# Delta-net substitution: its steps on GpSimd instead of VectorE, and the order they share with the key pages

## The chip, the cores and the metric

One core of a Trainium2 chip runs the whole kernel. The metric is the device time in microseconds (us), the median of several runs. The engines are named as the profile names them: PE is TensorE (matmuls), PEld its weight loads, DVE is VectorE, ACT is ScalarE, POOL is GpSimd, SP is SyncE, which only issues transfers here. ACTq and SPq are the transfer queues of ACT and SP.

## The reference, cut to what matters

One layer of a decoder: a normalised input goes through one projection, whose columns feed three kinds of heads (differential attention over paged keys and values, a state space model, a gated delta net) and their gates; the mixed result goes through an output projection. The change concerns the delta net, four heads of 128 over 1024 positions:

```python
lower = jnp.where(strict, beta[..., :, None] * kk * decay, 0.0)
rhs = jnp.concatenate([v * beta[..., None], k * (beta * jnp.exp(g_cum))[..., None]], axis=-1)
sol = lax.linalg.triangular_solve(lower + eye, rhs, left_side=True, lower=True, unit_diagonal=True)
u, w = sol[..., :DV_C], sol[..., DV_C:]
```

and, in the attention of the eight sample rows, the logits of a query against 4096 past keys each, which lie in pages of 128:

```python
logits = jnp.einsum('bqhmd,bkhmd->bmhqk', q, k).astype(jnp.float32) * (DH_A ** -0.5)
```

## The kernel before

**Stages.** From 0 to about 850 us the input projection runs (L458 in `proj_fm`). Each weight tile is split into a high part (`whi`, cast on ACT, L155) and a low part (`wlo`, a subtraction on POOL, L201), and each 128 columns of output take 72 matmuls in three pieces of positions, three for each of eight slices: high times high, high times low, low times high. The buffers of the split weights are three half tiles deep (`WB = 3`). Beside this run the sample attention (key and value pages stream in on SP's queue) and the delta-net heads 1 to 3. From 860 to 1100 us follow the prompt attention, head 4 of the delta net and the state space model, then the output projection (L1833).

**Key pages.** `k_pages` loads two pages into a tile `kt` (`KB = 3` buffers), multiplies them with the query on POOL (L842, four products of 128x256) and sums them on DVE (L843) into `lg`. `page_softmax` (L853, L858 and others, PE and DVE) follows when all pages of a sample are in, and `v_mul` (L898) multiplies value pages `vt` with the weights `wz`.

**A delta-net head** (`gdn_head`). The triangular system is solved for chunks of 128 positions. `LT` holds the matrices. Their 32x32 blocks on the diagonal are stored to memory (`invd`) and loaded again as `Dm`, one block to each partition group's row (L1131 to L1134, on ACT's queue). Then 31 steps invert them by substitution in the tile `U`: a product with a row of `Dm` into `tv`, and a subtraction, each on DVE through the helper `tt` (L159). `U` is stored (L1151) and loaded back into `LT` (L1154), again on ACT's queue, and PE goes on from there: transposes (L1163), the off-diagonal blocks (L1175 to L1199), the right-hand sides (L1207, L1208), and the recurrence over eight chunks (L1220 to L1226).

**What sets the order.** The kernel is written as generators that are advanced in turn by the cost they yield, and a planner then reorders the instructions of each engine by a timeline of its own. One rule is written by hand: `gstep` holds the last step written so far, and what `k_pages` issues inside `behind_gdn()` on the engine of that step is ordered behind it (`tc.issue_after` adds an order on one engine, no wait between engines). While the steps are on DVE, these are the reductions L843. An engine runs its instructions in the planned order.

Of the kernel before, what the change touches and what calls it, by code (L numbers as in the profile page):

```python
# [14 lines left out]
ALU = mybir.AluOpType  # L15
# [63 lines left out]
def bl(ap, n):  # L79
    return ap.unsqueeze(len(ap.shape)).broadcast_to(list(ap.shape) + [n])  # L80


def bm(ap, n):
    return ap.unsqueeze(1).broadcast_to([ap.shape[0], n] + list(ap.shape[1:]))
# [3 lines left out]
def trunk_kernel(  # L88
# [47 lines left out]
    def unit(shape, dt=F32, n="u"):  # L136
        return up.tile(shape, dt, tag="u", name=nm(n))

    def half(shape=(P, 512), dt=F32, n="h"):
        return hp.tile(list(shape), dt, tag="h", name=nm(n))  # L140
# [9 lines left out]
    def small(shape, n, dt=F32, bufs=2):  # L150
        return sp.tile(shape, dt, tag=n, name=nm(n), bufs=bufs)
# [6 lines left out]
    def tt(out, a, b, op):  # L158
        return V.tensor_tensor(out=out, in0=a, in1=b, op=op)  # L159
# [3 lines left out]
    def tte(e, out, a, b, op):  # L163
        return EN[e].tensor_tensor(out=out, in0=a, in1=b, op=op)
# [877 lines left out]
    def gdn_head(h):  # L1042
# [89 lines left out]
        Dm = unit([P, 32, 32], n="Dm")  # L1132
# [3 lines left out]
        U = half([P, 16, 32], n="U")  # L1136
# [6 lines left out]
        for j in range(31):  # L1143
            n, m = 31 - j, j // 4 + 1
            tv = U[:, 8:16].rearrange("p a b -> p (a b)")[:, 0:m * n].rearrange("p (c i) -> p c i", i=n)
            tt(tv, bl(U[:, 0:m, j], n), bm(Dm[:, j, j + 1:32], m), ALU.mult)
            step = tt(U[:, 0:m, j + 1:32], U[:, 0:m, j + 1:32], tv, ALU.subtract)
            gstep[:] = [step.ins]
            yield 0.5
        for g in range(4):  # L1150
# [86 lines left out]
        m = small([P, 8], "sm")  # L1237
# [370 lines left out]
    def gdn_all():  # L1608
        for h in range(4):
            while len(graw.get(h, ())) < 3:  # L1610
                yield 0.5
            yield from gdn_head(h)
# [58 lines left out]
    for b in range(32):  # L1671
        n = bk.count(b)
# [271 lines left out]
```

## Time and profile before

| | us |
|---|---|
| median of 3 runs | 1275.63 |
| lowest, highest | 1272.66, 1278.05 |
| profiled execution | 1270.58 |
| its span in the trace | 1268.8 |
| PE busy in the span | 1136.3 (90%) |
| DVE busy | 833.6 (66%) |
| POOL busy | 643.8 (51%) |
| ACT busy | 471.6 (37%) |

The profiled execution is one run of the same program; its stretches are read in us from the start of the span. PE is the engine with the most work. Its clock varies: the granted clock of the whole span is 0.947 of full speed in the mean. The four heads substitute at about 276 to 322, 481 to 532, 688 to 732 and 900 to 940 us.

### The profile page before, as it was taken

To read this page: it belongs to the slowest core of one execution; us is meant where nothing else is said; L and a number is where in the kernel's file an instruction comes from. 1 tells how busy PE (TensorE), PEld (TensorE's weight loads), DVE (VectorE), ACT (ScalarE), POOL (GpSimd) and SP (SyncE) were. 2 spreads that over 40 slices of the span, in tenths; PEclk is the share of its full clock that TensorE was granted. 3 is DMA by queue.
4 is the path that set the end of the run, shared out by engine and by line. 5 is a ranking of instruction groups with operands and counts; after the bars stand their busy time and mean duration, and the time that the engine had idled before them with its cause. 6 is when DMAs were issued, how large, how long until landed. Compare 5 with 4: busy or idle time off the path is not lost.

```text
span 1268.8 us, 22346 instructions
## 1 busy us (share of the span) xinstructions
PE 1136.3 (90%) x7365; PEld 959.4 (76%) x7365; DVE 833.6 (66%) x1994; ACT 471.6 (37%) x998; POOL 643.8 (51%) x779
## 2 busy tenths in 40 slices
PE   4999999989889988888997799988899999799997
PEld 3799887768669777867866688866568778678876
DVE  6723698549478658945754955787878988664444
ACT  6332223211114332233353233436737759341111
POOL 3747867646665653573965778772023251341100
PEclk9999999989789988898988899998998999899999
DMA  8646765994884962696797599999786664961420
GB/s 298 200 164 205 238 208 161 349 324 134 280 293 155 319 214 77 190 333 211 234 318 226 183 322 336 307 287 257 219 225 174 161 167 133 299 198 52 131 69 34
DMA packets 246452, 275.57 MB, mean 217 GB/s; under 512 B 31905, under 2 KB 163376, under 8 KB 246322
## 3 DMA queue, kind: packets, MB, share of 16 engines
q1 hardware_dynamic: 168082, 214.44, 52.3%
q10 hardware_dynamic: 78256, 59.72, 16.4%
q8 instruction: 58, 0.95, 0.3%
q14 instruction: 56, 0.46, 0.1%
HBM read 231.59 MB, written 42.67 MB: 216 GB/s over the span
## 4 chain that ended last, share of the span: by engine, by line
PE 53%; DMA 16%; DVE 15%; issue 5%; ACT 3%; SPq 3%; POOL 3%; ACTq 1%; DVEq 0%; POOLq 0%
PE b L458 23%; PE b L1833 10%; PE pv L898 4%; DMA kt<-in_cache_k_dram 3%; DVE U L159 3%; DMA vt<-in_cache_v_dram 3%; DMA w<-in_w_in_dram 2%; DVE lg L843 2%; DVE cy L167 2%; PE b L745 1%; SPq L823 1%; POOL kt L842 1%; PE b L1893 1%; DVE e L721 1%; DMA zb<-zfd 1%
## 5 line engine op out<-in xcount | busy, mean ns | idle before, releaser
L458 PE MATMUL b<-hh,whi 128*128 128x344 f32 (+1 forms) x2016 | 508.6, 335 | 23.0 <-DVE cy L167 11.6
L842 POOL TENSOR_TENSOR kt<-kt,qb 128x256 f32<-128x256 f32 x512 | 364.5, 745 | 159.8 <-DMA kt<-in_cache_k_dram 104.0
L458 PEld LDWEIGHTS b<-hh,whi 128*128 128x128 f32 x2016 | 363.7, 197 | 56.0 <-issue 30.1
L458 PE MATMUL b<-hh,wlo 128*128 128x344 f32 (+1 forms) x1008 | 332.4, 334 | 3.5 <-POOL wlo L201 3.5
L843 DVE TENSOR_REDUCE lg<-kt 128x16 f32<-128x1024 f32 x128 | 154.6, 1211 | 88.0 <-POOL kt L842 85.2
L458 PEld LDWEIGHTS b<-hh,wlo 128*128 128x128 f32 x1008 | 197.1, 196 | 15.7 <-issue 10.1
L201 POOL TENSOR_TENSOR wlo<-w,whi 128x512 fp32r<-128x512 f32 x86 | 111.1, 1297 | 92.9 <-ACT whi L155 80.5
L1833 PE MATMUL b<-wo,mh 128*128 128x512 f32 (+1 forms) x408 | 121.7, 380 | 0.2 <-POOL wo L1567 0.2
L155 ACT ACTIVATE whi<-w 128x512 fp32r<-128x512 f32 x86 | 54.1, 631 | 160.8 <-PE b L458 114.4
L167 DVE SCALAR_TENSOR_TENSOR cy<-b,vec,cy 128x341 f32<-128x341 f32 (+4 forms) x180 | 99.0, 563 | 1.5 <-DVE U L159 0.2
L898 PE MATMUL pv<-vt,wz 128*32 128x512 f32 x512 | 78.3, 645 | 22.6 <-DMA vt<-in_cache_v_dram 15.0
L1833 PEld LDWEIGHTS b<-wo,mh 128*128 128x128 f32 x408 | 74.6, 188 | 14.5 <-POOL wo L1567 0.4
L1833 PE MATMUL b<-wo,ml 128*128 128x512 f32 (+1 forms) x204 | 77.1, 378 | 0.0
L1801 POOL TENSOR_TENSOR ml<-zt,mh 128x512 fp32r<-128x512 f32 x16 | 22.4, 1404 | 104.7 <-ACT mh L1800 104.5
L159 DVE TENSOR_TENSOR U<-U,Dm 128x60 f32<-128x60 f32 (+24 forms) x124 | 40.6, 327 | 18.7 <-DMA Dm<-invd 16.8
L156 ACT ACTIVATE e<-e,nmx 128x128 f32<-128x128 f32 (+7 forms) x64 | 48.9, 766 | 8.8 <-DVE nmx L723 5.4
L155 ACT ACT_TABLE_LOAD x33 | 42.3, 1283 | 25.5 <-DMA qh<-qfd 8.5
L718 PE MATMUL b<-kTh,qh 128*128 128x128 f32 (+3 forms) x96 | 41.1, 431 | 11.7 <-DVE mx L721 6.5
L159 DVE TENSOR_TENSOR y<-b,gate 128x512 f32<-128x512 f32 (+1 forms) x17 | 11.1, 658 | 54.2 <-PE b L1833 54.2
L1833 PEld LDWEIGHTS b<-wo,ml 128*128 128x128 f32 x204 | 38.3, 188 | 7.3
L971 DVE TENSOR_SCALAR cy<-b,vec 128x344 f32<-128x344 f32 (+1 forms) x60 | 33.2, 564 | 14.5 <-PE b L458 14.3
L898 PEld LDWEIGHTS pv<-vt,wz 128*32 128x32 f32 x512 | 12.4, 110 | 39.6 <-issue 18.9
(531 smaller groups left out, 2022.9 us busy)
## 6 DMA issues: line engine op xcount, KB each, us to landing
kt<-in_cache_k_dram SPq DMA_DIRECT2D x256, 256.0 KB
vt<-in_cache_v_dram SPq DMA_DIRECT2D x256, 256.0 KB
w<-in_w_in_dram ACTq DMA_DIRECT2D x82, 256.0 KB
zfd<-zf ACTq DMA_DIRECT2D x12, 512.0 KB
wo<-in_w_out_dram SPq DMA_DIRECT2D x12, 512.0 KB
om<-mixd SPq DMA_DIRECT2D x24, 256.0 KB
xt<-in_x_prompt_dram SPq DMA_DIRECT2D x8, 512.0 KB
hx<-in_w_ada_dram SPq DMA_DIRECT2D x16, 256.0 KB
```

The costliest lines, as they stand in the source:

```text
L155: return S.activation(out, in_, func, bias=bias, scale=scale)
L156: return S.activation(out, in_, func, bias=bias, scale=scale, accum_out=accum)
L159: return V.tensor_tensor(out=out, in0=a, in1=b, op=op)
L167: return V.scalar_tensor_tensor(out=out, in0=a, scalar=s, in1=b, op0=op0, op1=op1)
L201: G.tensor_tensor(out=lo, in0=w32, in1=hi.bitcast(F32), op=ALU.subtract)
L458: TE.matmul(ps[:, 0:N], a, b[k][:, sl], start=(i == 0), stop=(i == 23))
L718: TE.matmul(ps[:, 0:b - a], qh[:, m, ts], kT[m][:, a:b], start=True, stop=False)
L842: G.tensor_tensor(out=kt[:, j, c], in0=kt[:, j, c], in1=qb[:, c], op=ALU.mult)
L843: V.tensor_reduce(out=lg[:, 2 * g:2 * g + 2, :], in_=kt.rearrange("p j (a d) -> p j a d", d=64), axis=AX.X, op=ALU.add)
L898: mm = TE.matmul(pv[32 * r:32 * r + 32, :], wz[:, 2 * g + j, :], vt[:, j, :], start=(b == 0 and g < 2), stop=(b == NS - 1 and g >= 14 and ...
L971: V.tensor_scalar_mul(y[:, c0_:c0_ + m], ps[:, o:o + m], wv[3])
L1833: TE.matmul(ps[c], m[a][:, kt % 4, :], w[kt][:, c[0]:c[1]], start=(kt == KT[0] and i == 0), stop=(kt == KT[-1] and i == 2))
```

## The change

The two instructions of each of the 31 steps are issued through the helper `tte` (L164) with engine "g", so on POOL, with the same operands: 248 instructions in four heads. `gstep` then holds an instruction of POOL, and what `behind_gdn()` orders behind it are the products L842 in the place of the reductions L843. Nothing else is written differently.

```diff
@@ -1143,8 +1143,8 @@
         for j in range(31):
             n, m = 31 - j, j // 4 + 1
             tv = U[:, 8:16].rearrange("p a b -> p (a b)")[:, 0:m * n].rearrange("p (c i) -> p c i", i=n)
-            tt(tv, bl(U[:, 0:m, j], n), bm(Dm[:, j, j + 1:32], m), ALU.mult)
-            step = tt(U[:, 0:m, j + 1:32], U[:, 0:m, j + 1:32], tv, ALU.subtract)
+            tte("g", tv, bl(U[:, 0:m, j], n), bm(Dm[:, j, j + 1:32], m), ALU.mult)
+            step = tte("g", U[:, 0:m, j + 1:32], U[:, 0:m, j + 1:32], tv, ALU.subtract)
             gstep[:] = [step.ins]
             yield 0.5
```

The planner answers with another order on all engines. On POOL, in head 1's substitution, the row before is this (`wlo` are low halves of weights, `kt` key pages, numbers tell tiles apart, `kN` is a scaling of the head's keys):

```order
L201 TENSOR_TENSOR wlo_3659<-w_473_3624,whi_3658 128x512
L842 TENSOR_TENSOR kt_3439<-kt_3439,qb_3265 128x256 x4
L201 TENSOR_TENSOR wlo_3746<-w_474_3626,whi_3745 128x512
L842 TENSOR_TENSOR kt_3500<-kt_3500,qb_3265 128x256 x4
L201 TENSOR_TENSOR wlo_3912<-w_502_3877,whi_3911 128x512
L842 TENSOR_TENSOR kt_3566<-kt_3566,qb_3265 128x256 x4
```

and now, near the end of the head's steps:

```order
L842 TENSOR_TENSOR kt_3268<-kt_3268,qb_3265 128x256 x4
L164 TENSOR_TENSOR U_2837<-U_2837,Dm_2832 128x48
L201 TENSOR_TENSOR wlo_3746<-w_474_3626,whi_3745 128x512
L164 TENSOR_TENSOR U_2837<-U_2837 128x6x8
L164 TENSOR_TENSOR U_2837<-U_2837,Dm_2832 128x49
L201 TENSOR_TENSOR wlo_3912<-w_502_3877,whi_3911 128x512
L164 TENSOR_TENSOR U_2837<-U_2837 128x7x7
L164 TENSOR_TENSOR U_2837<-U_2837,Dm_2832 128x42
L164 TENSOR_TENSOR U_2837<-U_2837 128x7x6
L164 TENSOR_TENSOR U_2837<-U_2837,Dm_2832 128x35
L164 TENSOR_TENSOR U_2837<-U_2837 128x7x5
L842 TENSOR_TENSOR kt_3357<-kt_3357,qb_3265 128x256 x4
```

The low halves and the products have moved in among the steps; behind wlo_3912 there are 15 more steps and the products of kt_3357 up to the head's last step. In head 2, wlo_5527 stands behind 26 steps in the same way.

On PE, where head 3's chain begins (`b` are accumulators; L458 is the projection, `pv` the products of value pages), the row before is

```order
L458 MATMUL b_8566<-hh_514,wlo_8393 128x344
L458 MATMUL b_8566<-hh_525,whi_8392 128x344
L1163 MATMUL b_8155<-ident,LT_7281 128x128 x4
L1163 MATMUL b_8163<-ident,LT_7281 128x128 x4
L898 MATMUL pv<-vt_8396,wz 32x512 x2
L898 MATMUL pv<-vt_8408,wz 32x512 x2
L458 MATMUL b_8566<-hh_526,whi_8392 128x344
L458 MATMUL b_8566<-hh_525,wlo_8393 128x344
```

and now

```order
L458 MATMUL b_8721<-hh_773,wlo_8478 128x344
L898 MATMUL pv<-vt_8076,wz 32x512 x2
L898 MATMUL pv<-vt_8144,wz 32x512 x2
L898 MATMUL pv<-vt_8222,wz 32x512 x2
L898 MATMUL pv<-vt_8338,wz 32x512 x2
L1163 MATMUL b_8155<-ident,LT_7281 128x128 x4
L1163 MATMUL b_8163<-ident,LT_7281 128x128 x4
L1175 MATMUL b_8202<-T_973_7472,LT_7281 32x32 x4
L1176 MATMUL b_8203<-T_973_7472,LT_7281 32x32 x4
```

The transposes L1163 have moved from behind 2620 to behind 2688 matmuls of L458, and the chain from L1163 to L1226 now stands in a row, with products of value pages but no projection matmuls between. In head 1 the transposes stand behind 1176 matmuls of L458 in both orders, and the chain stood in a row there already.

## Rows read from the trace of the kernel before

**Rows 1.** The page, busy us (share of the span) and instructions of two engines.

```profile
PE 1136.3 (90%) x7365; PEld 959.4 (76%) x7365; DVE 833.6 (66%) x1994; ACT 471.6 (37%) x998; POOL 643.8 (51%) x779
```

**Rows 2.** The page, the chain that ended last, share of the span by line.

```profile
PE b L458 23%; PE b L1833 10%; PE pv L898 4%; DMA kt<-in_cache_k_dram 3%; DVE U L159 3%; DMA vt<-in_cache_v_dram 3%; DMA w<-in_w_in_dram 2%; DVE lg L843 2%; DVE cy L167 2%; PE b L745 1%; SPq L823 1%; POOL kt L842 1%; PE b L1893 1%; DVE e L721 1%; DMA zb<-zfd 1%
```

**Rows 3.** Windows: stretch, length, busy us by engine, granted clock, DMA share, GB/s.

```profile
core 0: us, PE busy (x) PEld busy (x) DVE busy (x) ACT busy (x) POOL busy (x), PEclk, DMA share, GB/s
276.00:322.00 46.00, 43.90 (x265) 36.41 (x258) 41.06 (x112) 7.76 (x13) 20.52 (x24) 1.00 0.64 200
332.00:368.00 36.00, 25.62 (x215) 15.79 (x213) 17.21 (x28) 8.27 (x21) 23.43 (x33) 0.70 0.85 295
481.00:532.00 51.00, 46.41 (x265) 43.94 (x266) 47.23 (x127) 10.79 (x14) 22.78 (x26) 0.88 0.38 118
692.00:732.00 40.00, 31.59 (x167) 29.89 (x166) 38.30 (x86) 10.20 (x16) 27.20 (x31) 0.83 0.61 194
732.00:760.00 28.00, 28.00 (x255) 23.77 (x253) 12.37 (x15) 11.75 (x23) 23.84 (x30) 1.00 1.00 324
900.00:940.00 40.00, 35.44 (x242) 22.39 (x242) 34.29 (x162) 16.35 (x47) 4.54 (x8) 1.00 0.82 241
```

**Rows 4.** Windows of tile U alone, four heads' substitutions: sum and mean.

```profile
sum 181.00, DVE 77.05 POOL 0.00; mean DVE 19.26 POOL 0.00
```

**Rows 5.** Timeline of DVE: start, us, line, operation [idle before <- releaser].

```profile
276.19 0.18 DVE L159 TENSOR_TENSOR U<-U,Dm 128x31 f32<-128x31 f32 x1
...
321.15 0.16 DVE L159 TENSOR_TENSOR U<-U 128x8 f32<-128x8 f32 x1
...
481.21 0.19 DVE L159 TENSOR_TENSOR U<-U,Dm 128x31 f32<-128x31 f32 x1 [2.64 <-DMA Dm<-invd]
...
688.07 0.19 DVE L159 TENSOR_TENSOR U<-U,Dm 128x31 f32<-128x31 f32 x1 [14.15 <-DMA Dm<-invd]
...
731.14 0.17 DVE L159 TENSOR_TENSOR U<-U 128x8 f32<-128x8 f32 x1
...
936.95 0.68 DVE L159 TENSOR_TENSOR pvs<-pv,hm 128x512 f32<-128x512 f32 x1
```

**Rows 6.** Timeline of PE: its stops on DVE, and head 1's and 3's transposes.

```profile
317.60 0.55 PE L458 MATMUL b<-hh,whi 128*128 128x344 f32 x2 [1.57 <-DVE U L159]
...
334.20 1.06 PE L1163 MATMUL b<-ident,LT 128*128 128x128 f32 x8 [1.83 <-DMA LT<-invd]
...
511.16 0.91 PE L458 MATMUL b<-hh,whi 128*128 128x344 f32 x2 [3.37 <-DVE cy L167]
...
700.24 0.27 PE L853 MATMUL b<-ident,smx 128*8 128x128 f32 x1 [2.02 <-DVE U L159]
...
709.59 0.59 PE L858 MATMUL b<-sdg,ones 8*128 8x8 f32 x2 [3.62 <-DVE sdg L857]
...
727.45 1.08 PE L898 MATMUL pv<-vt,wz 128*32 128x512 f32 x8 [2.78 <-DVE wz L159]
...
749.33 1.03 PE L1163 MATMUL b<-ident,LT 128*128 128x128 f32 x8
```

**Rows 7.** Groups of POOL by form: count, busy us, mean ns, idle before.

```profile
L842 POOL TENSOR_TENSOR kt<-kt,qb 128x256 f32<-128x256 f32 x512 | 364.5, 745 | 159.8 <-DMA kt<-in_cache_k_dram 104.0 <-DVE U L159 12.8 <-DMA qb<-qd 10.7
L201 POOL TENSOR_TENSOR wlo<-w,whi 128x512 fp32r<-128x512 f32 x86 | 111.1, 1297 | 92.9 <-ACT whi L155 80.5 <-PE b L1119 9.7 <-PE b L458 1.4
```

**Rows 8.** Timeline of POOL: a memset and two small copies.

```profile
938.27 0.31 POOL L1497 MEMSET gwz<- 128x256 f32 x1 [1.96 <-PE b L1501]
938.64 0.33 POOL L1499 COPY gwz<-gWQ 128x8 f32<-128x8 f32 x2
```

**Rows 9.** Windows of line L458 alone on PE: matmuls up to two times.

```profile
0.00:743.00 743.00, 463.56 (x2588) 0.93 0.72 232
0.00:316.50 316.50, 194.29 (x1104) 0.97 0.71 228
```

**Rows 10.** Timeline of ACT and its queue: the store of U in head 1.

```profile
321.35 2.64 ACTq L1151 DMA_DIRECT2D invd<-U  x4
```

## What I expect, and how I come to it

> **What bounds the kernel now.** I read the busy shares first. TensorE is busy for 90% of the span, GpSimd for 51% [rows 1], so the time is that of TensorE's work plus the places where it stands still or runs at its lower clock. The chain of work that ended last, by line, puts 23% on the projection matmuls L458 and only 3% on the steps (VectorE, tile U, L159) [rows 2]: some 40 us of 1268.8 are at stake in the steps, and not all of that can be had.
>
> The busy time by stretches says where. While heads 1, 2 and 3 substitute (276 to 322, 481 to 532, 692 to 732 us), VectorE is busy 41.06 of 46, 47.23 of 51 and 38.30 of 40 us: it is the tight engine there. GpSimd has 20.52, 22.78 and 27.20 us of work in the same stretches, so it isn't idle either [rows 3]. The steps themselves take 77.05 us of VectorE in four heads, 19.26 each [rows 4], and from first to last step a head takes about 45 us, because VectorE does other work between them (276.19 to 321.15 in head 1 [rows 5]).
>
> **What the change takes off VectorE.** The waits of TensorE that name VectorE in the three stretches are the gain. Head 1: one wait of 1.57 us on a step. Head 2: 3.37 us on the convolution's VectorE work, which stands in the queue between steps [rows 6], and 2.64 us in which VectorE itself stood at the first step, waiting for Dm, with convolution work queued behind it [rows 5]. Head 3: 2.02, 3.62 and 2.78 us, all three in the page softmax and its weights, whose VectorE work stands among steps [rows 6]; sum 8.4. Each such stop is followed by matmuls at a lower granted clock: it is 0.83 over 692 to 732 and 0.88 over 481 to 532, against 1.00 where nothing stops [rows 3]. A mean of 0.83 between the two levels (1.2 and 2.4 GHz) is a third of 40 us, 13 us, at the low one, where a matmul takes nearly twice as long; that loses about 6 us in head 3, and I take 2 in head 2, where part of the low clock comes from a stop that stays. Gains: head 1 1.6, head 2 2.64 + 3.37 + 2 = 8.0, head 3 8.4 + 6 = 14.4. Head 4's steps (in 900 to 940) are half of VectorE's 34.29 us there, and TensorE is idle for 4.6 of 40 us [rows 3]; I take half, 2 us. All gains: 26 us.
>
> **What a step costs on GpSimd.** No row shows a small two-input instruction there. The nearest are the products of 256 elements a partition at 745 ns and the low halves of weights (wlo, L201) of 512 at 1297 ns [rows 7]; the line through both is 2.16 ns an element and 193 ns. The 62 instructions of a head have 50 elements in the mean (31 steps of (31-j) columns by j//4+1): 302 ns. A copy that follows a memset starts 0.06 us after the memset's end (938.27 + 0.31 to 938.64) [rows 8], and every step waits for the one before, so 0.36 us and 62 x 0.36 = 22.4 us a head. From below: two copies of 8 elements took 0.33 us [rows 8], 0.17 each, with the gap 0.23, 14.3 us a head. From above: twice VectorE's 19.26 us, 38.5 us a head, 0.62 each. I take 0.36, since it is read off the same operation on the same engine, and keep the ends.
>
> **What the steps stand between on GpSimd.** With the new order, from the first step of a head to its last GpSimd also runs 23, 27 and 41 instructions of its other work, by the mean times of their groups 21.6, 24.6 and 39.3 us (products, wlo, kN, in head 3 the state's products too). With 22.4 us of steps that is 44.0, 47.0 and 61.7 us from first to last. VectorE needed 45.0 (276.19 to 321.15) in head 1 and 43.1 (688.07 to 731.14) in head 3 [rows 5]. The steps haven't become shorter, then; in head 3 they end later by 18.6 us, at 749.8.
>
> **Head 1.** GpSimd runs in order, so each wait of its other work now holds the substitution. wlo_3912 stands with 15 steps and the products of kt_3357 behind it. Its buffer comes free when TensorE ends the 1104th matmul of L458; in the trace that is at 316.50 [rows 9]. From there 1.3 (wlo) + 4 x 0.745 + 15 x 0.36 = 9.7 us: the last step at 326.2, where it was 321.3. Then U is stored and LT loaded back: the store is issued at 321.35 [rows 10], and the transposes L1163 begin at 334.20, 12.9 us after the last step, already waiting for LT by 1.83 us [rows 6]. Nothing covers a delay there: +4.9 us, which takes the 1.57 us with it. By the low price of a step it is +3.0; by the high one the sum of the work decides, 276.2 + 21.6 + 38.5 = 336.3, +15.
>
> **Head 2.** The steps end by 47.0 us after 481.2, earlier than before, so LT isn't late. But wlo_5527 stands behind 26 of the steps, and TensorE's matmuls on it with it: between nothing and 26 x 0.36 = 9.4 us, depending on how far GpSimd is ahead of TensorE there, which no row settles. I take half: 8.0 gained, 4.7 lost, -3.3.
>
> **Head 3.** U's end at 749.8 and 12.9 us for the way through memory give LT at 762.7. In the trace L1163 runs at 749.33 behind 2620 matmuls of L458 [rows 6], and 2588 of them had run by 743 [rows 9], 0.20 us each with all that stands between; in the new order 2688 stand ahead of it, 68 more, 13.6 us. Less the 14.4 us gained TensorE gets there at 748.5 and waits 14.2 us. Behind it the whole chain of head 3 now stands in a row, without projection matmuls between its members. Head 1 shows what this costs: over 332 to 368 us, where its chain runs so, TensorE is busy 25.62 of 36 us at a granted clock of 0.70, while head 3's, which is interleaved now, runs with 28.00 of 28 us busy at 1.00 [rows 3]. So 10 us are lost that aren't lost now (the clock, which would add to it, I leave out, and keep it for the range). Head 3: -14.4 + 14.2 + 10 = +9.8.
>
> **The order rule.** The rule that held VectorE's reductions L843 behind the last step written ahead of them now holds GpSimd's products L842 there; both stand on the engine of the steps, so no wait across engines is added, only places in a queue (counted above). The reductions are free of it, which may hand key buffers back to the page loads on SP's queue sooner; against that stand products that come later in head 3, where the DMA share is 1.00 in 732 to 760 already [rows 3]. I put no number on either.
>
> **Sum:** 4.9 - 3.3 + 9.8 - 2 = +9.4 us on the profiled execution's 1270.58, 1280.0. That execution lies 5.05 us below the median of the three runs, 1275.63; on the median the forecast is 1285.0.
>
> **The rivals.**
> 1. Faster: GpSimd is quick on small tiles and the wait at L1163 is short. At 0.23 us a step: head 1 +3.0; head 2 -8.0, nothing late; head 3 ends at 688.1 + 39.3 + 14.3 = 741.7, LT at 754.6, a wait of 6.1 us and, with the clock kept up, half the 10 us: -3.3; head 4 -2. Sum -10.3: 1265. For it speaks that the 8-element copies are that short; against it, the line through the same operation and that the wait on wlo_3912 doesn't depend on a step's price. It decides if U of head 3 ends by about 742 us in terms of the old trace.
> 2. No change: the price is 0.36, but ScalarE's cast for wlo_3912 comes early enough (head 1: 0) and the serial block of head 3 loses 5 us less: 0 - 3.3 + 4.8 - 2 = -0.5, 1275. For it: pv products stand between the members of that block and fill some of it.
> 3. Much slower: the steps cost 0.62 us. Head 1 +15; head 2 -8.0 + 26 x 0.62 / 2 = 0; head 3: U at 688.1 + 39.3 + 38.5 = 765.9, LT at 778.8, a wait of 30.3 us, +25.9; head 4 -2. Sum +39: 1315. The 38.5 us are twice the trace's 19.26, in which contention with GpSimd is already contained [rows 4]; the line through the two rows on GpSimd [rows 7] speaks against it.
>
> On rival 3 there is a rule. The Trainium skill, "GPSIMD Engine Reference", section 4.1 Engine selection, names VectorE for elementwise work on a tile and puts GpSimd at about twice its time for operations with two inputs. At 512 elements the trace agrees: VectorE took 0.68 us for a product [rows 5], GpSimd 1.297 us for wlo [rows 7]; no row shows it at 50 elements. By the rule the time would be rival 3's, 1315.
>
> **How the numbers follow.** Forecast 0.40, rival 1 0.22, rival 2 0.25, rival 3 0.13. About 0.5% (6 us) is what a measurement of this kernel can tell from no change. The forecast and rival 3 are slower by more than that (0.53), rival 1 faster (0.22), rival 2 within it (0.25). The range reaches into rival 1, to 1261, and to just short of rival 3's full price, 1312; what is left out is about half of each, 0.18.
>
> **What would show it.** The mean distance of two steps on GpSimd in the profile after: 0.36 right, 0.25 rival 1, 0.6 rival 3. TensorE's wait at L1163 for LT: about 7 us in head 1 and 14 in head 3 if I am right, 2 and 6 by rival 1. TensorE's waits on VectorE in the page softmax of head 3 should be gone, and its granted clock in the step stretches near 1.00. The chain should show GpSimd's steps L164 in head 3 in the place of VectorE's L159. The forecast is wrong if GpSimd's own waits (on pages, on ScalarE's casts) stand still less than I think, or if the time lost in head 3's block comes back in the page stream that has to end anyway.

## The result: 1.3% slower

| | before | after |
|---|---|---|
| median, us (4 runs each) | 1276.84 | 1291.06 |
| lowest, highest | 1272.66, 1281.92 | 1290.51, 1294.70 |
| profiled execution | 1270.58 | 1290.51 |
| its span | 1268.8 | 1288.8 |

The ratio is 1.0126, with an interval of 1.0091 to 1.0160. The two profiled executions are 20 us apart, the medians 14; the kernel before varies by some 10 us from run to run, and its profiled one is a quick one. So a difference read from the two traces may be 6 us too large.

The page of the kernel after, its busy shares and its chain by line (to be read against [rows 1, 2]):

```profile
PE 1142.6 (89%) x7365; PEld 959.1 (74%) x7365; DVE 771.3 (60%) x1746; ACT 469.9 (36%) x997; POOL 720.3 (56%) x1027
...
PE b L458 24%; PE b L1833 10%; DMA vt<-in_cache_v_dram 4%; PE pv L898 4%; POOL kt L842 2%; DVE lg L843 2%; DMA kt<-in_cache_k_dram 2%; POOL U L164 2%; DVE cy L167 1%; PE b L745 1%; POOL wlo L201 1%; SPq L823 1%; ACT e L156 1%; DMA hx<-in_w_ada_dram 1%; PE b L1893 1%
```

VectorE has lost 62 us of work and GpSimd gained 76; on the chain the steps now stand as POOL U L164, and the key products on GpSimd rose to 2%. The stretches of the kernel after (columns as in [rows 3]): head 1's steps and the block behind them, head 2's steps, head 3's steps and the block behind them.

```profile
279.00:327.00 48.00, 48.00 (x290) 41.37 (x290) 25.86 (x50) 11.50 (x16) 39.55 (x87) 1.00 0.58 181
334.00:372.00 38.00, 24.43 (x202) 16.85 (x206) 17.43 (x24) 6.36 (x17) 25.28 (x36) 0.59 0.86 287
478.00:536.00 58.00, 52.59 (x313) 47.62 (x314) 38.16 (x78) 16.29 (x22) 45.10 (x95) 0.94 0.38 113
690.00:751.00 61.00, 57.12 (x349) 54.87 (x348) 25.39 (x42) 22.82 (x33) 56.82 (x104) 0.97 0.54 167
751.00:791.00 40.00, 30.12 (x236) 19.76 (x237) 15.88 (x18) 10.28 (x23) 32.42 (x46) 0.66 0.94 307
```

While a head substitutes, TensorE runs as it was meant to: busy 48.00 of 48 and 57.12 of 61 us, its granted clock 0.94 to 1.00. GpSimd is the full engine now, 56.82 of 61 us in head 3. What is lost is lost behind the steps: 751 to 791 us, 30.12 of 40 us busy at a clock of 0.66, where the kernel before ran with 28.00 of 28 at 1.00 [rows 3]. Of the 9.88 us in which TensorE stands there, nearly all lie ahead of the block, before 763.37; in the block itself it is busy for 26.48 of 27.63 us, and what it lacks is the clock. The two parts in the kernel after, and below them the times of the second in the kernel before:

```profile
751.00:763.37 12.37, 3.64 (x17) 0.42 (x17) 3.66 (x3) 0.63 (x1) 12.37 (x18) 0.58 0.88 248
763.37:791.00 27.63, 26.48 (x224) 19.33 (x221) 12.21 (x15) 9.65 (x22) 20.05 (x30) 0.69 0.98 334
```

```profile
763.37:791.00 27.63, 27.63 (x209) 24.43 (x207) 15.31 (x22) 10.51 (x19) 23.19 (x30) 1.00 1.00 337
```

Where in the program the time goes is seen best by counting the projection's matmuls (L458), as [rows 9] does. The time at which each was reached, in whole us:

| matmul of L458 | before | after | difference |
|---|---|---|---|
| 1176 (before head 1's block) | 332 | 330 | -2 |
| 1200 (behind it) | 373 | 381 | +8 |
| 1560 (shortly before head 2's steps) | 460 | 469 | +9 |
| 1992 (head 2 done) | 584 | 585 | +1 |
| 2400 (early in head 3's steps) | 697 | 698 | +1 |
| 2688 | 767 | 751 | -16 |
| 2712 (behind head 3's block) | 778 | 791 | +13 |
| 3024 (the last is the 3048th) | 843 | 859 | +16 |

In each head the steps' stretch gains, and the block behind it takes more than that back in heads 1 and 3. The count flatters the gain at the 2688th, though: the kernel before has by then also run 104 matmuls of head 3's chain and 32 of value pages that the kernel after still has ahead of it. They take 7.5 us in the trace before, so of the 17 us from the 2400th to the 2688th about 9 are gained, and 7.5 of what the block loses is work that was only moved. TensorE in the kernel after, at the two blocks (start us, us, line, operation [idle before <- releaser]):

```profile
337.93 1.30 PE L1163 MATMUL b<-ident,LT 128*128 128x128 f32 x5 [5.52 <-DMA LT<-invd]
...
752.83 1.77 PE L898 MATMUL pv<-vt,wz 128*32 128x512 f32 x8 [1.89 <-issue]
761.50 1.93 PE L898 MATMUL pv<-vt,wz 128*32 128x512 f32 x8 [6.90 <-DMA vt<-in_cache_v_dram]
763.37 1.97 PE L1163 MATMUL b<-ident,LT 128*128 128x128 f32 x8
```

In head 1 the transposes wait 5.52 us for LT. In head 3 TensorE comes to the products of value pages that stand ahead of L1163 at 751, has no page, and loses its 6.90 us there; LT is on its way in the same time, and L1163 itself doesn't wait. The loads of LT:

```profile
757.29 1.87 ACTq L1154 DMA_DIRECT2D LT<-invd  x4
```

That a value page was missing points to the second loss. SP's queue in the kernel after, and what it waited for between 711 and 745 us (waited for: us in total, times, longest):

```profile
711.63 1.02 SPq L823 DMA_DIRECT2D kt<-in_cache_k_dram  x2
719.65 0.40 SPq L1416 DMA_DIRECT2D out_dram<-sst  x1
737.68 0.86 SPq L823 DMA_DIRECT2D kt<-in_cache_k_dram  x2
739.14 0.86 SPq L823 DMA_DIRECT2D vt<-in_cache_v_dram  x2
```

```profile
SPq L823 <- DVE lg L843: 24.3, 2, 17.4
```

No page was asked for from 711.63 to 737.68: the key buffers were full, their products stood among steps on GpSimd, and the reductions that free the buffers waited for the products. On GpSimd, two neighbouring groups of products (steps and other work between):

```profile
707.53 2.82 POOL L842 TENSOR_TENSOR kt<-kt,qb 128x256 f32<-128x256 f32 x4
...
733.58 2.81 POOL L842 TENSOR_TENSOR kt<-kt,qb 128x256 f32<-128x256 f32 x4
```

The kernel before had a stop of its own, shorter and earlier: its loads waited 15.5 us for a step on VectorE, behind which the reductions are ordered, until 714 us. From there on it asked for pages all the time. The wait, and the same queue there:

```profile
SPq L823 <- DVE U L159: 15.5, 1, 15.5
...
722.46 1.20 SPq L823 DMA_DIRECT2D kt<-in_cache_k_dram  x2
723.90 0.97 SPq L823 DMA_DIRECT2D vt<-in_cache_v_dram  x2
728.72 0.85 SPq L823 DMA_DIRECT2D kt<-in_cache_k_dram  x2
730.16 0.86 SPq L823 DMA_DIRECT2D vt<-in_cache_v_dram  x2
```

What all transfers had moved by 840 us, in the last column as a mean in GB/s, first in the kernel before, then in the kernel after:

```profile
0.00:840.00 840.00, 749.64 (x5013) 646.91 (x5014) 540.52 (x1080) 267.28 (x458) 537.44 (x682) 0.94 0.75 243
```

```profile
0.00:840.00 840.00, 738.99 (x4893) 633.90 (x4894) 471.19 (x866) 267.53 (x455) 577.06 (x846) 0.93 0.73 234
```

Counted in packets these are 203.72 and 196.56 MB: 7.2 MB less, and at the 324 GB/s of a stretch in which the transfer engines are full [rows 3] 22 us of transfers, about the 20 us that the trace is longer. Up to 711 us both kernels have moved the same (231 GB/s). Half of the shortfall comes from 711 to 751 us, in the stop and just behind it, and half only from 751 to 840, where the transfer engines of the kernel after were busy for 0.94 and 0.87 of the time, those of the kernel before for 1.02 and 0.96 (751 to 791 and 791 to 840 us). From 840 to 900 us the kernel after moves 311 GB/s against 247 and gets some 4 MB back. The last product of a value page ran at 934.7 us before and at 958.8 after.

### The profile page after: what moved, and what is told of

Read it like the earlier page. It is cut to its first block, busy times and chain, and to the rows that moved or that the text cites. A ratio compares the mean times of both kernels' runs of the same rounds, so it can differ in the third digit from the quotient of the medians.

```text
span 1288.8 us, 22328 instructions
## 1 busy us (share of the span) xinstructions
PE 1142.6 (89%) x7365; PEld 959.1 (74%) x7365; DVE 771.3 (60%) x1746; ACT 469.9 (36%) x997; POOL 720.3 (56%) x1027
## 4 chain that ended last, share of the span: by engine, by line
PE 54%; DMA 16%; DVE 12%; POOL 6%; ACT 4%; issue 4%; SPq 3%; ACTq 1%; POOLq 0%; DVEq 0%
PE b L458 24%; PE b L1833 10%; DMA vt<-in_cache_v_dram 4%; PE pv L898 4%; POOL kt L842 2%; DVE lg L843 2%; DMA kt<-in_cache_k_dram 2%; POOL U L164 2%; DVE cy L167 1%; PE b L745 1%; POOL wlo L201 1%; SPq L823 1%; ACT e L156 1%; DMA hx<-in_w_ada_dram 1%; PE b L1893 1%
## 5 line engine op out<-in xcount | busy, mean ns | idle before, releaser
L458 PE MATMUL b<-hh,whi 128*128 128x344 f32 (+1 forms) x2016 | 502.8, 332 | 16.1 <-DVE cy L167 8.9
L842 POOL TENSOR_TENSOR kt<-kt,qb 128x256 f32<-128x256 f32 x512 | 365.1, 746 | 98.5 <-DMA kt<-in_cache_k_dram 72.3
L458 PEld LDWEIGHTS b<-hh,whi 128*128 128x128 f32 x2016 | 359.7, 195 | 39.5 <-issue 20.3
L458 PE MATMUL b<-hh,wlo 128*128 128x344 f32 (+1 forms) x1008 | 330.6, 332 | 8.0 <-POOL wlo L201 8.0
L843 DVE TENSOR_REDUCE lg<-kt 128x16 f32<-128x1024 f32 x128 | 154.9, 1213 | 145.4 <-POOL kt L842 138.2
L458 PEld LDWEIGHTS b<-hh,wlo 128*128 128x128 f32 x1008 | 195.5, 195 | 24.0 <-issue 12.6
L898 PE MATMUL pv<-vt,wz 128*32 128x512 f32 x512 | 80.9, 658 | 25.1 <-DMA vt<-in_cache_v_dram 20.8
L164 POOL TENSOR_TENSOR U<-U,Dm 128x60 f32<-128x60 f32 (+24 forms) x124 | 37.9, 306 | 45.1 <-DMA Dm<-invd 37.4
L898 PEld LDWEIGHTS pv<-vt,wz 128*32 128x32 f32 x512 | 12.7, 111 | 43.3 <-issue 21.0
L164 POOL TENSOR_TENSOR U<-U 128x60 f32<-128x60 f32 (+24 forms) x124 | 39.9, 322 | 8.1
```

What stands on the lines that cost most here:

```text
L458: TE.matmul(ps[:, 0:N], a, b[k][:, sl], start=(i == 0), stop=(i == 23))
L842: G.tensor_tensor(out=kt[:, j, c], in0=kt[:, j, c], in1=qb[:, c], op=ALU.mult)
L843: V.tensor_reduce(out=lg[:, 2 * g:2 * g + 2, :], in_=kt.rearrange("p j (a d) -> p j a d", d=64), axis=AX.X, op=ALU.add)
L898: mm = TE.matmul(pv[32 * r:32 * r + 32, :], wz[:, 2 * g + j, :], vt[:, j, :], start=(b == 0 and g < 2), stop=(b == NS - 1 and g >= 14 and ...
```

## Experiments

Theory at the start: head 3's block in a row costs most, head 1's a little, and head 2 gains. Rival A: the order of the key products behind the steps costs the time. Rival B: each head loses about the same, because GpSimd is full. All twelve runs, with the start of the last projection matmul on a high half of weights and of the last product of a value page in the trace (us); each run's ratio is to executions of the kernel before taken beside it:

| run | median | ratio to before (interval) | last L458 | last L898 | span |
|---|---|---|---|---|---|
| before | 1276.84 | | 846.9 | 934.7 | 1268.8 |
| after | 1291.06 | 1.0126 (1.0091 to 1.0160) | 863.3 | 958.8 | 1288.8 |
| e1 | 1292.66 | 1.0128 (1.0072 to 1.0184) | 856.1 | 951.5 | 1282.7 |
| e2 | 1283.07 | 1.0042 (1.0013 to 1.0072) | 862.7 | 958.1 | 1281.8 |
| e3 | 1351.56 | 1.0583 (1.0526 to 1.0640) | 929.7 | 1019.1 | 1350.1 |
| e4 | 1293.72 | 1.0131 (1.0068 to 1.0194) | 862.8 | 947.1 | 1291.1 |
| e5 | 1282.71 | 1.0052 (1.0014 to 1.0090) | 818.1 | 954.0 | 1279.8 |
| e6 | 1307.66 | 1.0254 (1.0193 to 1.0315) | 858.5 | 970.6 | 1315.1 |
| e7 | 1281.09 | 1.0036 (0.9996 to 1.0077) | 849.5 | 947.1 | 1284.6 |
| e8 | 1282.94 | 1.0034 (1.0001 to 1.0068) | 857.1 | 947.3 | 1287.6 |
| e9 | 1297.57 | 1.0187 (1.0144 to 1.0230) | 850.1 | 949.1 | 1292.2 |
| e10 | 1267.80 | 0.9922 (0.9892 to 0.9952) | 837.3 | 936.9 | 1268.3 |
| e11 | 1277.35 | 1.0035 (1.0000 to 1.0071) | 828.2 | 928.0 | 1272.6 |
| e12 | 1289.32 | 1.0082 (1.0050 to 1.0114) | 866.0 | 966.5 | 1293.7 |

**e1 and e2: the steps moved in head 3 alone, and in all heads but 3.** The helper's engine is chosen by head, here for e1:

```diff
-            tte("g", tv, bl(U[:, 0:m, j], n), bm(Dm[:, j, j + 1:32], m), ALU.mult)
+            tte("g" if h == 2 else "v", tv, bl(U[:, 0:m, j], n), bm(Dm[:, j, j + 1:32], m), ALU.mult)
... (the subtraction in the same way)
```

> The steps run on GpSimd in head 3 alone; heads 1, 2 and 4 have them on VectorE. In TensorE's order head 3's chain stands in a row here too (behind 2688 matmuls of L458, as in the changed kernel), heads 1 and 2 stand as before. Theory (most of the loss is head 3's block in a row): between the kernel before and the changed one by most of the difference, +10 to +18 us, about 1290; head 3's block costs TensorE 25 us and more. Rival B (each head loses about the same, because GpSimd is full): a third, +5 us, 1282. Rival A (the order of the key products behind the steps costs the time): about a third as well, since it holds in one head only.

> The steps run on GpSimd in heads 1, 2 and 4, on VectorE in head 3; there head 3's chain is interleaved with projection matmuls as before (75 of them between its first transposes and its right-hand sides). Theory: within 5 us of the kernel before, about 1277, what head 1 loses in its block head 2 gains. Rival B: +10 us, 1287. Rival A: +8 to +10 us.

Head 3 alone loses as much as the whole change, 1.0128 against 1.0126; the other three lose a third of it. Rivals A and B wanted a third of the loss in head 3 and two thirds in the others. By the count of matmuls, e1 is 24 us ahead of the kernel before at the 2688th and 1 us behind at the 2712th: its block costs 25 us, as in the kernel after (29 us), the 7.5 us of moved work included in both, and a wait of 7.39 us for a value page ahead of it. So the place of the loss is shown: most of it comes with head 3's steps. That it is the block in a row, and not the pages, isn't shown by these two, since both come with the same move.

**e3: the steps on GpSimd, nothing ordered behind them.**

```diff
-        if gstep:
+        if False:
             with tc.issue_after(gstep[0]):
```

> All steps on GpSimd as in the changed kernel, but nothing is ordered behind them: the products of key pages go where the planner puts them. In TensorE's order the chains of heads 1, 2 and 3 then all stand in a row. Rival A (the order costs the time): faster than the changed kernel by 8 us and more, 1275 to 1283. Theory (blocks in a row cost the time): not faster than the changed kernel, 1290 to 1305, with a second block in head 2.

Rival A falls: without the order the kernel is 60 us slower than with it, far above my range of 1290 to 1305 too. The products run ahead (the 160th at 323 us, 349 in the kernel after), the steps end late, and TensorE stands at the transposes of three heads. The waits of TensorE in e3:

```profile
PE b L1163 <- DMA LT<-invd: 61.6, 3, 27.2
```

**e4: the kernel before without its order.** The same edit, steps on VectorE.

> The kernel before without its order of VectorE's reductions behind the steps. In TensorE's order head 2's chain loses most of its interleaving, head 3's keeps it. Theory: +3 to +10 us, 1280 to 1286, by head 2's block, and the steps finish later, since reductions come in among them. Rival A (such an order holds the page stream up): faster than the kernel before by 3 us and more.

The order is worth 17 us on VectorE too, more than expected. The half of the change that carries the order along to the engine of the steps is the half without which the other would cost some five times as much.

**e5 and e6: the block in a row taken apart.** In the planned order the gate projections behind the 2688th matmul come only after the copy of the chain's first output tile o, in both kernels. With o in LT's buffer, which is dead by then, the planner puts projection matmuls between the members of the chain:

```diff
-        o = unit([P, 8, P], n="oC")
+        o = LT
```

> The changed kernel (all steps on GpSimd), with the output tile o of a head kept in the buffer of LT, which is dead by then, so one large tile fewer a head. In the planned order of TensorE the chains of heads 1 and 3 now have 90 and 103 projection matmuls between their first transposes and their right-hand sides, where the changed kernel has none. Theory (the chains in a row cost the time, about 10 us in head 1 and 25 in head 3): 25 to 35 us faster than the changed kernel, 1256 to 1266. Rival C (GpSimd's load and the late LT cost the time, the block is only where it shows): within 6 us of the changed kernel, 1285 to 1297, with waits at L1163 for LT in its place.

> The kernel before (steps on VectorE), with o in LT's buffer. Chains interleaved in heads 1, 2 and 3 (93, 105, 104 matmuls). Theory: head 1's block goes, 8 to 12 us faster than the kernel before, about 1267; then steps on GpSimd (the run with the same edit) are level with steps on VectorE within 6 us or ahead. Rival C: no change, 1277, and steps on GpSimd stay 10 us and more behind.

e5 does where it was aimed what was expected, and more: at the 2712th matmul it is 50 us ahead of the kernel before, and its projection ends at 818.1 us, 45 us earlier than that of the kernel after. The time falls by 8 us only. Its first and last times of the projection and of the value products:

```profile
L458 PE MATMUL b<-hh,whi x2016: 313/321/656, 69.7 to 818.1; 128*128 128x344 f32 x127, 128*128 128x348 f32 x57
...
L898 PE MATMUL pv<-vt,wz x512: 589/617/1063, 216.4 to 954.0; 128*32 128x512 f32 x171
```

The last value page is multiplied at 954.0, 5 us earlier than in the kernel after. So the block is a cause of the late projection, and here a projection that ends 45 us earlier was worth little; that this is so because pages end late is the reading that fits, not one that e5 shows. e6 missed on the other side: 31 us slower than the kernel before. Its projection is 22 us ahead at the 1992nd matmul and behind at the end, and its pages end at 970.6 (its trace is the slowest of five executions, 9 us above their median). What falls behind there was not tried. Of rival C, that the block is only where GpSimd's load shows, e5 leaves half: the block goes and the projection with it, and the time hardly follows.

**e7: low halves of the weights on VectorE.**

```diff
-        G.tensor_tensor(out=lo, in0=w32, in1=hi.bitcast(F32), op=ALU.subtract)
+        V.tensor_tensor(out=lo, in0=w32, in1=hi.bitcast(F32), op=ALU.subtract)
```

> The changed kernel with the low halves of the weights (L201) on VectorE, so that nothing TensorE's projection needs stands among the steps on GpSimd. Head 3's chain still stands almost in a row (behind 2687 matmuls, 1 between), head 1's too. If the wait for low halves behind steps costs the time (my terms of 4.9 us in head 1 and 4.7 us in head 2): 8 to 10 us faster than the changed kernel, 1282. Theory (blocks): the blocks' part stays, and with low halves that wait for VectorE within 6 us of the changed kernel.

10 us faster than the kernel after. That is the expectation from my terms, but not by their way: TensorE waits for low halves no less (9.4 us, against 8.0 in the kernel after). What is gone is their time on GpSimd among steps and products, and the last value page comes 12 us earlier.

**e8: the steps moved in head 4 alone.**

> The steps on GpSimd in head 4 alone, with TensorE's order in heads 1 to 3 as before. My term: -2 us. By the last stage of the changed kernel's trace, which loses 4 us between the end of the projection and the end: +4 us. Both are near what can be measured; VectorE's waits on itself in the prompt attention should fall.

My gain of 2 us is not there: 1.0034 is 4 us slower, with an interval that just leaves out no change. Its profiled execution is 10 us behind that of the kernel before at the 2592nd matmul already, with head 4 still to come and TensorE's order in heads 1 to 3 as before, so head 4 alone can't be read from it more closely.

**e9 to e12: the exchange.** New theory P: in head 3 the pages fall behind, the transfer engines can't catch up, and the last stage waits for the pages. While a head substitutes on GpSimd, the key products written meanwhile go to VectorE, which the steps have left:

```diff
-    gstep = []
+    gstep = []; gact = [-1]
...
-                    G.tensor_tensor(out=kt[:, j, c], in0=kt[:, j, c], in1=qb[:, c], op=ALU.mult)
+                    (V if gact[0] >= 0 else G).tensor_tensor(out=kt[:, j, c], in0=kt[:, j, c], in1=qb[:, c], op=ALU.mult)
...
-        gstep.clear()
+        gstep.clear(); gact[0] = h
...
-        kb = unit([P, 8, P], n="kb")
+        kb = unit([P, 8, P], n="kb"); gact[0] = -1
```

e9 does it for head 3 alone (`gact[0] == 2`), e10 for all heads, e11 adds e5's edit, and e12 makes the same edit in the kernel before.

> The changed kernel, with the products of key pages that are written while head 3 substitutes on VectorE instead of GpSimd; the steps stay on GpSimd. In TensorE's order head 3's chain is then interleaved again (behind 2633 matmuls, 55 between). Theory P (what costs the time is that key pages fall behind in head 3, by 33 us at the 384th product in the changed kernel, and can't catch up, and the last stage waits for the pages): the 384th product within 10 us of the kernel before, the last product of value pages 15 us earlier than in the changed kernel, 1272 to 1280. If the low halves behind steps cost most of it: no more than 5 us faster than the changed kernel, 1286 and above.

> The same for all four heads: while a head substitutes on GpSimd, the key products written meanwhile are on VectorE. Chains interleaved in heads 1 to 3. Theory P: pages on time or ahead in all heads, 8 us and more faster than the kernel before, 1260 to 1270, ahead of both kernels. Theory of blocks alone: the projection ends 25 us earlier and the time falls by as much, 1250.

> The same again, with o in LT's buffer, so that the chains are interleaved more (89, 110 and 95 matmuls to the right-hand sides, against 61, 105 and 57). Theory P: a lead of the projection is worth nothing while pages are late, so within 6 us of the run before it in this list. Theory of blocks: 8 us and more faster than that run.

> The kernel before (steps on VectorE), with the key products that are written while a head substitutes on VectorE too. It tells what the faster run owes to the exchange of the two and what to the move of the products alone. If the exchange is needed (VectorE is 83 to 96% busy in the three stretches and would get some 90 products of half a microsecond more): slower than the kernel before by 8 us and more, 1283 to 1300. If the move of the products alone is what helps: 1270 and below, level with the exchange.

e10 is faster than both kernels, 0.9922 of the kernel before and 23 us faster than the kernel after. Its stretch up to 840 us (columns as in [rows 3]), and its own step stretches of heads 1 to 3, which end earlier than those of the kernel before:

```profile
0.00:840.00 840.00, 753.86 (x5060) 642.50 (x5060) 535.44 (x994) 267.23 (x458) 536.74 (x780) 0.96 0.75 244
280.00:315.00 35.00, 31.34 (x175) 26.63 (x172) 23.89 (x48) 6.62 (x11) 27.34 (x70) 0.92 0.78 252
476.00:501.00 25.00, 18.21 (x104) 18.12 (x105) 17.40 (x41) 5.80 (x8) 20.38 (x65) 0.79 0.42 135
675.00:723.00 48.00, 42.39 (x250) 40.98 (x249) 22.97 (x35) 14.42 (x21) 39.98 (x82) 0.93 0.56 166
```

Neither VectorE nor GpSimd is full in them: in head 3 VectorE has 22.97 of 48 us, where it had 38.30 of 40 before [rows 3], and GpSimd 39.98, where it had 56.82 of 61 in the kernel after. By 738 us 386 pages have been asked for, 380 in the kernel before and 363 in the kernel after, and by 840 us the transfers have moved what the kernel before had. 92 products moved; they take 513 ns each on VectorE in the mean (416 in the median), against 756 (738) for those that stayed on GpSimd:

```profile
L842 POOL TENSOR_TENSOR kt<-kt,qb 128x256 f32<-128x256 f32 x420 | 302.3, 756 | 104.5 <-DMA kt<-in_cache_k_dram 77.7 <-DMA qb<-qd 11.8 <-DVE sto L159 4.2
L842 DVE TENSOR_TENSOR kt<-kt,qb 128x256 f32<-128x256 f32 x92 | 42.1, 513 | 9.6 <-DMA kt<-in_cache_k_dram 6.8 <-DMA qb<-qd 2.8
```

The pages are not all that e10 changes. In its order the chains of heads 1 and 3 are interleaved again, with 61 and 57 projection matmuls between the first transposes and the right-hand sides, where the kernel after has none; e5, with 90 and 103, gained 8 us by that alone. So some of the 23 us may be the chains'. Nor are the moved products ordered behind the steps any more, since the rule orders on the engine of the steps alone.

In e12 the same move, with the steps left on VectorE, is slower than the kernel before, 1.0082: the move alone doesn't pay. But there products and reductions both stand on the engine of the steps, so the rule holds both back, and TensorE's order is another (head 2's chain in a row, 36 matmuls in head 3's instead of 68, and 7.39 us of waiting for LT in head 1 instead of 1.83), so that VectorE's load is the reason isn't shown. e11 fits neither theory: against e10 its projection and its last value page both end 9 us earlier, and the time is 10 us longer.

Nor does e9. Key pages are on time (the 96th pair of pages is reduced at 679 us, at 698 in the kernel before and 712 in the kernel after), the chain is interleaved, the projection ends 13 us earlier than in the kernel after, the last value page 10 us earlier (15 were expected), and the time is no shorter: 1.0187 against 1.0126. Head 3's block and head 3's late pages are both gone, and the loss is not, though the last value page is still 14 us later than in the kernel before. What both lose, they lose late. In e9, from the last value page to the first matmul of the output projection it takes 181 us (949.1 to 1129.8), in e11 182; in the kernel before it takes 170 (934.7 to 1104.5), in the kernel after 166 and in e10 168. In all runs this distance lies between 161 and 183 us, in two groups (161 to 170 in before, after, e1, e2, e3, e5, e10, e12; 175 to 183 in e4, e6 to e9 and e11), whatever the change in the projection is. The planner orders the last stage anew each time, and some orders are some 15 us worse; what in them is worse stays open, and with it how much of e9's loss belongs to the change.

What the runs say together: the span less the time of the last value product is 324 to 345 us in all fourteen traces; less the time of the last projection matmul it is 419 to 462. The end follows the pages more closely than the projection, and most closely within each of the two groups of the last stage. The last value page also lies 88 to 136 us nearer to the end, so part of that is to be expected.

## Why the prediction was right, and where not

The forecast was +9.4 us and 1285.0, the measured medians are +14.2 and 1291.06, in the range; the direction and its chief place, head 3, were right. The terms behind the sum were not all: several are off by 5 us and more, and they cancel. Point by point:

- **What a step costs: right.** Two pieces of head 1's steps on GpSimd in the kernel after:

```profile
307.17 0.32 POOL L164 TENSOR_TENSOR U<-U,Dm 128x75 f32<-128x75 f32 x1
307.57 0.34 POOL L164 TENSOR_TENSOR U<-U 128x75 f32<-128x75 f32 x1
...
325.70 0.22 POOL L164 TENSOR_TENSOR U<-U 128x16 f32<-128x16 f32 x1
326.00 0.20 POOL L164 TENSOR_TENSOR U<-U,Dm 128x8 f32<-128x8 f32 x1
326.28 0.21 POOL L164 TENSOR_TENSOR U<-U 128x8 f32<-128x8 f32 x1
```

  0.40 us from one to the next at 75 elements and 0.30 at 8 to 16, around the 0.36 read off the line through the two large forms. In the mean it is 0.39 us wherever two steps follow each other directly. Four heads' steps take 78 us of GpSimd; they took 77.05 of VectorE [rows 4]. Rival 3 is refuted at this size: a step of 31 elements follows its predecessor by 0.31 us (279.12 to 279.43) on GpSimd, and by 0.22 on VectorE with nothing between (276.19 to 276.41), 1.4 times. The rule of twice the time by the Trainium skill ("GPSIMD Engine Reference", 4.1 Engine selection) does not hold for such small tiles; the larger ones come near it. At 256 elements the key products of e10 take 738 ns in the median on GpSimd and 416 on VectorE, 1.8 times, and at 512 the low halves take 1286 in the kernel before and 693 on VectorE in e7, 1.9 times (min/median/max):

```profile
L842 POOL TENSOR_TENSOR kt<-kt,qb x420: 718/738/1829, 104.3 to 866.5; 128x256 f32<-128x256 f32 x140
L842 DVE TENSOR_TENSOR kt<-kt,qb x92: 403/416/2114, 250.2 to 693.3; 128x256 f32<-128x256 f32 x92
L201 DVE TENSOR_TENSOR wlo<-w,whi x86: 668/693/7652, 5.0 to 834.0; 128x512 fp32r<-128x512 f32 x86
```

- **Head 1, the wait on wlo_3912 with 15 steps behind: right in place and size.** wlo_3912 waits 0.78 us and the last step ends at 326.5, forecast 326.2. The wait at L1163 is 5.52 us, forecast about 7. But the block behind it runs slower than before, at 0.59 instead of 0.70, so head 1 costs 8 us at the 1200th matmul, not 4.9. The stop of 1.57 us that was to go with it stands in a stretch at 1.00 [rows 3, 6]; that each stop is followed by a lower clock holds in heads 2 and 3, not here.
- **Head 2: the loss of 4.7 is not there.** From +9 to +1 us, a gain of 8, which is the size of the gains in the sum without the loss beside them, though not made up as there. Between the 1560th and the 1992nd matmul TensorE stands 14.6 us instead of 17.9 (its two longest waits on the convolution's VectorE work are 3.02 and 1.55 us, 6.14 and 3.37 before), and most of the rest is the granted clock, 0.96 instead of 0.92. TensorE's waits on low halves rose from 3.5 to 8.0 us in the whole trace, but none lies in this stretch; GpSimd was ahead there and waited 17.33 us for ScalarE's cast at 479.8 us.
- **Head 3: right in place and nearly in sum, not in its terms.** The steps take 60.0 us from first to last (690.73 to 750.73), forecast 61.7. From the 2400th to the 2712th matmul the kernel after goes from +1 to +13, 12 us lost where the sum had 9.8. The gain was about 9 us, forecast 14.4: the waits on VectorE are gone, but one on a low half has come, which the sum had in heads 1 and 2 only:

```profile
704.50 0.43 PE L458 MATMUL b<-hh,wlo 128*128 128x344 f32 x1 [3.79 <-POOL wlo L201]
```

  Ahead of L1163 TensorE stood 8.8 us (1.89 and 6.90), forecast 14.2, and not for LT: both waits are ahead of products of value pages, the longer for a page. The sign that was named, 14 us at L1163 for LT, did not show. The 10 us that the block was to stand still are 1.2 us. In their place the block ran at the lower clock, which the sum left out and the range kept: a mean of 0.69 between the two levels is 17 of 27.6 us at the low one, some 9 us lost by my estimate. So a term of the right size came by another way, and that the sum is close is luck. e1 loses 25 us in its block, nearly as much, with the steps moved in this head alone.
- **The order rule, "I put no number on either": the step that failed.** The products "that come later in head 3" held SP's page loads up for 26 us, where the kernel before held them up for 15.5. By 840 us 7.2 MB were missing, half of them lost behind the stop, and the last value page came 24 us late. The reductions, set free of the order, gave nothing back: they wait for the products (138.2 us in the trace after, 85.2 before). I had priced TensorE's path alone and set the page stream aside as having no sure sign. e5 took 45 us off the projection and 8 off the time; e10, which gives the products another engine and interleaves the chains again, takes back the whole loss and 9 us more.
- **Head 4: a gain of 2 us that isn't seen.** From +16 us at the last projection matmul to +20 at the end in the two traces, 4 us in e8, neither sure beyond the spread of the runs.

So the sum was nearly right for the wrong balance: a gain too large, a wait too long, a loss in head 2 that didn't come and a clock that was left out cancel, and beside TensorE's path the page stream, which has no term at all, ends late by more than the whole forecast. How much of the 14 us belongs to the pages and how much to TensorE's block stays open. That the stream alone sets the end is not shown: it is inferred from the order of the ends in all traces and from e5 and e10, and e9 and e11 speak against it unless their last stage is set apart.

## To carry to other kernels

When work moves to an engine that is half idle, price what else stands in that engine's queue, and follow whose buffers it frees: here key products, behind them reductions, behind them page loads, and a transfer stream that caught up only in part. Count matmuls to see where time goes, but compare at places where both orders have done the same work. Two streams can end a kernel side by side; if they do, a gain on one is worth only the distance to the other, so price both before adding up the waits on the first. Moving the chain paid here when work left the engine it goes to: the exchange was worth 23 us against the move alone, a part of it perhaps through TensorE's order.

## What the runs showed of the hardware that was not expected

On small tiles GpSimd is close to VectorE: 248 dependent operations of 50 elements in the mean took 78 us of the one and 77 of the other in this kernel's company, though with nothing between them VectorE is 1.4 times as fast. VectorE's price depends on the head: 17.61, 19.05, 25.82 and 14.78 us for the same 62 instructions in heads 1 to 4 of the kernel before. GpSimd was busiest beside the third (27.94 of 44 us) and least beside the fourth (4.54 of 40); whether that is the reason was not tried. And a one-line change of a buffer (e6), to which the planner answered with another order, cost 2.5%; what in that order costs it was not tried.
